# Six small reorderings in a diffusion-transformer layer: a load on another queue, three pieces of work on another engine or copied first, two steps turned later

## The chip, the core and the metric

The kernel runs on one core of a Trainium2 chip. The metric is the device time of one execution in microseconds (us), the median of repeated runs; lower is better. The engines are TensorE (PE in the profile, its weight loads PEld), VectorE (DVE), ScalarE (ACT), GpSimd (POOL) and SyncE (SP, which here only issues DMAs). L12 is line 12 of the kernel.

## What is computed

One layer for 1024 latent tokens and 256 context tokens of width 1024, in float32:

```python
h_lat = rms_norm(x, norm1_g) * (1.0 + sc1) + sh1        # sc1, sh1, ... = silu(c) @ w_mod + b_mod
h_ctx = rms_norm(ctx, norm1_g) * (1.0 + csc1) + csh1
p = h @ w_in                                            # 7 blocks of 512 columns
# retention: 4 heads of 128, both directions, chunks of 128, state carried from chunk to chunk
scores = (qc @ kc.T) * intra; o = scores @ vc + (qc * q_dec) @ S; S = S * c_dec + (kc * k_dec).T @ vc
# differential attention: 4 heads, two maps of 64; keys are the context and the latent tokens (1280)
a = softmax(q1 @ k1.T) - lam * softmax(q2 @ k2.T); y = subln(a @ v)
x = x + g1 * (concat(silu(rg) * ret, y) @ w_out)
u = conv3(h2 @ w_up); a, b = split(u); x = x + g2 * ((silu(a) * b) @ w_down)   # d_ff 2816, taps along the tokens
return rms_norm(x, final_g)
```

## The kernel before

Every matmul of a projection is done in three passes on values split into a high part (rounded to the faster format fp32r) and the remaining low part: high by high, high by low, low by high (`passes`, L131 to L133). The high part is cast by ScalarE, the low part is a subtraction, mostly on VectorE. In some stretches (the opening, the attention) the order of each engine's instructions is that of the code (`in_order`); elsewhere a scheduler orders them by readiness, and `order_only` adds a fixed precedence of one instruction to another of the same engine. In a queue a waiting instruction holds all behind it.

**Opening.** The rows of x come in on one DMA queue or another (`load_row`), the modulation weights in pieces (`mod_load`, tile wt), the projection's weights by blocks of two 128-row slices (`w_load`, tile raw, split by `w_split` into whi and wlo). A row is squared on ScalarE, its factor raised to −1/2 on GpSimd (`power`), scaled on VectorE (`scale`, L542), turned by TensorE into pt (L548), and `modulate(xs, d, ...)` writes the high part on ScalarE (L551), a temporary on VectorE (L553) and the low part (L555) for the 128-row slice d. `mod_part`, `mod_row` and `mod_sums` make the modulation itself: products into pr (L520), and small sums into pm and mcol. `part_products(ts, k)` multiplies slice k for the token tiles ts into pn. `turn_over(n)` issues n small products on ones (L606). Context tokens run through the same steps (cT).

**Retention.** `outputs()` is a generator that is run beside the q projection's products (pl, L131 to L133). A pair is two chunks of a head. In step n the pair n + 1 gets its scores, pair n its outputs (po) and the squares for its group norm (jk, ss on ScalarE, the power on GpSimd), pair n − 1 its gating (`gate`: four scalings o on VectorE, then y on GpSimd at L280 and L281), and pair n − 3 is turned by TensorE (`turn`: pyt, L286), split (yr) and stored (yrd, L291, on SP's queue). Behind the last y GpSimd issues the loads of the attention's operands (qhl, ks, va; L947 to L953).

**q items.** Each product block of q or k (bank pl) goes through `rotated`: ScalarE copies the two halves crosswise to xb (L423), VectorE multiplies pl by the cosine to xa (L425), then xb by the sine (L426, on GpSimd for the last items) and adds (L427). The attention is woven in before the last q items are done: scores pA (L868), row maxima on VectorE (L871), exponential on ScalarE (L875), transposes of p into pt (L888), which takes a bank of the same pool as pl, and copies aT (L894).

**Gated MLP.** Blocks j of 128 hidden columns are 2 by 2 products of Strassen's kind, accumulated in the bank `chain` in steps T2, T3, T4, with copies between them (ua at L1285, ub at L1293 and L1301, all on ScalarE); banks `second`, `third` and `fifth` hold further products. `combined(j)` makes the sums of weight tiles (cmb): s3 alone for the first blocks, on GpSimd (L1196). `conv` is the tap of width 3: the middle on ScalarE (L1238), the neighbours on VectorE (L1239, L1240), then SiLU (L1306). In blocks 1 to 3 (`late_gate`) the gating of the block before is issued after the middle of this one.

## Time and profile before

| | before |
|---|---|
| median of 3 runs | 1391.22 us (1389.7 to 1391.42) |
| profiled execution | 1391.29 us |
| its span, first to last instruction | 1389.5 us |
| mean granted TensorE clock | 0.998 |
| TensorE busy | 1363.6 us, 98% |
| VectorE, ScalarE, GpSimd busy | 996.3, 731.9, 306.2 us |

In rows of the timeline the first number is the start in us from the span's start, the second the length, then engine, line, operation and tiles; x6 after a row says that six such instructions run there one after the other; the bracket holds the idle time before the row and what ended it.

### The profile page before, as it was taken

The numbers are of one execution on the slowest core, as the hardware profiler recorded it, in microseconds if no ns is written. First come the engines' busy times: TensorE is split into PE (matmuls) and PEld (weight loads), VectorE is DVE, ScalarE is ACT, GpSimd is POOL, SyncE is SP. The second block draws the span as 40 slices with busy tenths as digits, with TensorE's granted clock in tenths as the row PEclk, the third lists the DMA queues.
The fourth block names the chain that finished last, engine by engine and source line by source line (L and its number), as shares of the span: only waits on it lengthen the run. The fifth ranks groups of instructions, "written<-read, shape, count | busy, mean of one in ns | idle before, by whom it ended". The sixth has DMA issues, their size and how long they took to land. (4 is left out here: it accounts for less than half of the span.)

```text
span 1389.5 us, 19442 instructions
## 1 busy us (share of the span) xinstructions
PE 1363.6 (98%) x7038; PEld 1145.9 (82%) x7038; DVE 996.3 (72%) x1464; ACT 731.9 (53%) x1395; POOL 306.2 (22%) x327
## 2 busy tenths in 40 slices
PE   8999999999999999999999999999999999999997
PEld 5788888888888899998887788888888888888886
DVE  4656773424776798895458998888778877798757
ACT  4652222424665789987136654555544555455542
POOL 1310000002655424411201643222332220000001
PEclk9999999999999999999999999999999999999999
DMA  9546885464454778622410232332322325963523
GB/s 367 207 167 214 286 280 180 142 178 141 152 187 149 205 178 184 139 51 99 171 64 23 99 113 100 114 114 93 112 104 109 114 75 177 371 220 104 175 91 129
DMA packets 94760, 214.61 MB, mean 154 GB/s; under 512 B 9221, under 2 KB 29189, under 8 KB 94153
## 3 DMA queue, kind: packets, MB, share of 16 engines
q1 hardware_dynamic: 85928, 186.64, 39.1%
q0 software_dynamic: 8160, 24.91, 7.9%
q10 hardware_dynamic: 576, 1.84, 0.4%
q8 instruction: 55, 0.90, 0.3%
q14 instruction: 41, 0.33, 0.1%
HBM read 158.03 MB, written 55.31 MB: 154 GB/s over the span
## 5 line engine op out<-in xcount | busy, mean ns | idle before, releaser
L131 PE MATMUL pl<-hT,whi 128*128 128x512 f32 x256 | 105.7, 413 | 0.0
L131 PE MATMUL chain<-T,whi 128*128 128x512 f32 x264 | 103.0, 391 | 1.2 <-ACT ub L1293 0.8
L132 PE MATMUL chain<-T,whi 128*128 128x512 f32 x264 | 102.7, 389 | 0.0
L133 PE MATMUL chain<-T,wlo 128*128 128x512 f32 x264 | 102.4, 389 | 0.0
L133 PE MATMUL pl<-hT,wlo 128*128 128x512 f32 x256 | 100.3, 392 | 0.3 <-DVE wlo L188 0.3
L132 PE MATMUL pl<-hT,whi 128*128 128x512 f32 x256 | 100.0, 391 | 0.0
L871 DVE TENSOR_REDUCE mt<-pA 128x1 f32<-128x1280 f32 x64 | 95.1, 1490 | 3.7 <-PE pA L868 2.3
L131 PE MATMUL c<-whi,ghl 128*128 128x512 f32 x232 | 90.2, 389 | 0.0
L132 PE MATMUL c<-wlo,ghl 128*128 128x512 f32 x232 | 90.2, 389 | 0.0
L133 PE MATMUL c<-whi,ghl 128*128 128x512 f32 x232 | 90.2, 389 | 0.0
L868 PE MATMUL pA<-ks,qhl 128*128 128x512 f32 (+1 forms) x384 | 89.5, 369 | 0.3 <-ACT p L875 0.3
L875 ACT ACTIVATE p<-pA,mt 128x1280 f32<-128x1280 f32 x64 | 85.5, 1336 | 6.2 <-DVE mt L871 6.1
L1039 ACT CAST whi<-cmb 128x512 fp32r<-128x512 f32 x62 | 38.5, 622 | 80.5 <-PE chain L132 63.0
L868 PEld LDWEIGHTS pA<-ks,qhl 128*128 128x128 f32 x384 | 67.7, 189 | 12.7 <-ACT p L875 1.0
L900 PE MATMUL pv<-va,aT 128*128 128x128 f32 x640 | 77.0, 275 | 0.1
L131 PE MATMUL pn<-whi,hT 128*128 128x512 f32 x188 | 76.8, 408 | 0.0
L1199 POOL TENSOR_TENSOR cmb<-wrb 128x512 f32<-128x512 f32 x19 | 27.6, 1452 | 221.9 <-DMA wrb<-w_up 132.0
L1042 DVE TENSOR_TENSOR wlo<-cmb,whi 128x512 fp32r<-128x512 f32 x62 | 61.0, 985 | 20.4 <-ACT whi L1039 20.4
L133 PE MATMUL pn<-whi,hT 128*128 128x512 f32 x188 | 73.7, 392 | 1.3 <-POOL hT L555 1.2
L900 PEld LDWEIGHTS pv<-va,aT 128*128 128x128 f32 x640 | 74.0, 192 | 0.7 <-DVE yT L929 0.3
L132 PE MATMUL pn<-wlo,hT 128*128 128x512 f32 x188 | 73.7, 392 | 0.8 <-DVE wlo L578 0.8
L1039 ACT CAST whi<-wra 128x512 fp32r<-128x512 f32 x55 | 33.8, 623 | 74.5 <-PE third L132 42.3
(326 smaller groups left out, 3824.3 us busy)
## 6 DMA issues: line engine op xcount, KB each, us to landing
wm<-w_mod SPq DMA_DIRECT2D x32, 512.0 KB, 5.3
raw<-w_in SPq DMA_DIRECT2D x27, 512.0 KB, 4.6
wra<-w_up SPq DMA_DIRECT2D x24, 512.0 KB, 3.3
wrb<-w_up SPq DMA_DIRECT2D x22, 512.0 KB, 3.5
W<-w_down SPq DMA_DIRECT2D x44, 256.0 KB, 6.0
ad<-s SPq DMA_DIRECT2D x20, 512.0 KB, 3.6
wra<-ad SPq DMA_DIRECT2D x20, 512.0 KB, 3.8
kvs<-kvg SPq DMA_DIRECT2D x36, 256.0 KB, 3.0
```

Source lines behind the costliest of these rows:

```text
L131: mm(ps, lh, rh, start=first, stop=False, skip_group_check=more)
L132: mm(ps, lh, rl, start=False, stop=False, skip_group_check=more)
L133: mm(ps, ll, rh, start=False, stop=last, skip_group_check=more)
L868: mm(self.pa[m][:, c0:c1], self.q[:, m, i, qs], self.k[:, m, c0:c1], start=(i == 0), stop=(i == 1))
L871: nc.vector.tensor_reduce(out=self.mt[:, m : m + 1], in_=self.pa[m][:, :LK], axis=AX.X, op=ALU.min)
L875: nc.scalar.activation(self.p[m], self.pa[m][:, :LK], AF.Exp, scale=-1.0, bias=self.mt[:, m : m + 1], accum_out=self.s[:, m : m + 1])
L900: mm(self.pv, self.aT[:, c, :], self.v[:, c, :], start=(c == 0), stop=(c == NKT - 1))
L1039: cast = nc.scalar.copy(hi, src)
L1042: nc.vector.tensor_tensor(out=lo, in0=src, in1=r32(hi), op=ALU.subtract)
L1199: nc.gpsimd.tensor_tensor(out=s1, in0=b1, in1=b2, op=ALU.add)
```

## The change

Six edits. (1) In the opening, row 1 of x goes to SP's queue and the first half of the projection's first weight block to ScalarE's; rows are scaled in two pieces of 3/4 and 1/4; the slices after the first are multiplied pass by pass over two token tiles, as the first was; the splits of weights stand ahead of the squares of the second group of rows; the count of small filler products changes. (2) The low part of slice 1 is made on VectorE, not GpSimd, for latents and context. (3) `turn` stands one step later in `outputs()`, behind the pair's outputs and squares, and the last one two steps later still. (4) The last q item's bank is copied whole by ScalarE into an SBUF tile before it is rotated. (5) s3 of block 1 is made on VectorE. (6) In blocks 1 to 3 the first tap of the gating is ordered behind the copy of the third chain step.

```diff
@@ outputs()
-                if 0 <= n - 3 < n_pairs:
-                    pairs[n - 3].turn()
                 if 0 <= n < n_pairs:
                     pairs[n].output(1)
                     pairs[n].squares()
                 yield
+                if n == n_pairs + 2:
+                    yield
+                    yield
+                if 0 <= n - 3 < n_pairs:
+                    pairs[n - 3].turn()
                 if 0 <= n - 1 < n_pairs:
                     pairs[n - 1].gate()
@@ rotated()
             xb = ev.tile([P, 512], F32, name="xb")
+            if eng is nc.gpsimd and (h, hf) == by_head[-1]:
+                held = ev.tile([P, 4, P], F32, name="st").rearrange("p h e -> p (h e)")
+                nc.scalar.copy(held, pt)
+                pt = held
@@ modulate()
-                eng = nc.gpsimd if d % 2 else nc.vector
+                eng = nc.gpsimd if d % 2 and d > 1 else nc.vector
@@ part_products()
-                if k > 0:
-                    for t in ts:
-                        passes(part[t], lat_lhs(t, k), wget(k, 0, 512), False, k == KD - 1)
-                    return
                 hi, lo = wget(k, 0, 512)
...
@@ opening
-            for t in range(2):
-                load_row(t, nc.scalar)
+            load_row(0, nc.scalar)
+            w_load(0, 0, 1, nc.scalar)
+            nc.sync.dma_start(out=ident, in_=consts[:, K_ID : K_ID + P])
+            load_row(1)
             mod_load(0, 1)
-            nc.sync.dma_start(out=ident, in_=consts[:, K_ID : K_ID + P])
-            w_load(0, 0, 1)
...
-            turn_over(2)
+            turn_over(9)
             mod_part(0, 1)
...
-            mod_row(0)
-            mod_sums(0)
-            scale(xs0[0], 2)
-            turn_over(6)
+            scale(xs0[0], 2, 0, 3 * P)
             square(xs0[1], 3)
             power(3)
+            mod_row(0)
             w_split(0, 1, nc.scalar)
-            scale(xs0[1], 3, 0, 2 * P)
+            scale(xs0[1], 3, 0, 3 * P)
+            mod_sums(0)
+            turn_over(1)
...
                 if k == 1:
                     mod_sums(2)
                     latents(0, 2)
+                    for t in (2, 3):
+                        scale(xs0[t], 2 + t, 3 * P, D)
...
+                if k in (0, 2, 4):
+                    w_split()
                 if k == 3:
                     square(xs1[0], 6)
                     square(xs1[1], 7)
...
-                if k in (0, 2, 4):
-                    w_split()
@@ combined()
-            nc.gpsimd.tensor_tensor(out=s3, in0=b2, in1=a1, op=ALU.subtract)
+            (nc.vector if j else nc.gpsimd).tensor_tensor(out=s3, in0=b2, in1=a1, op=ALU.subtract)
@@ conv() and gated()
-        def conv(u, idx):
+        def conv(u, idx, after=None):
...
-            nc.scalar.activation(t, u, AF.Identity, scale=w[1], bias=cl[:, COL_CB + idx : COL_CB + idx + 1])
+            mid = nc.scalar.activation(t, u, AF.Identity, scale=w[1], bias=cl[:, COL_CB + idx : COL_CB + idx + 1])
+            if after is not None:
+                order_only(mid.ins, after.ins)
...
-                ta = conv(self.ua, self.j)
+                ta = conv(self.ua, self.j, after and copied[-1])
```

The line numbers of the new kernel lie 3 to 7 higher than those above. On TensorE, at the last two outputs of retention (po the outputs of the last pair, pl products of the q projection, pyt a turn), the order before is this:

```order
L263 MATMUL po<-S_3513,qq 128x128
L131 MATMUL pl<-hT_167,whi 128x512
L132 MATMUL pl<-hT_169,whi 128x512
L133 MATMUL pl<-hT_167,wlo 128x512
L286 MATMUL pyt<-ident,y 128x128 x2
L262 MATMUL po<-kvo,sc 128x128
L263 MATMUL po<-S_3512,qq 128x128
```

and now:

```order
L131 MATMUL pl<-hT_167,whi 128x512
L132 MATMUL pl<-hT_169,whi 128x512
L133 MATMUL pl<-hT_167,wlo 128x512
L262 MATMUL po<-kvo,sc 128x128
L263 MATMUL po<-S_3515,qq 128x128
L262 MATMUL po<-kvo,sc 128x128
L263 MATMUL po<-S_3516,qq 128x128
L131 MATMUL pl<-hT_167,whi 128x512
L132 MATMUL pl<-hT_169,whi 128x512
L133 MATMUL pl<-hT_167,wlo 128x512
L286 MATMUL pyt<-ident,y 128x128 x2
```

The turn that stood ahead of the pair's second outputs stands three products behind them. Of the turns that follow, 15, 12 and 15 products stood before, between and ahead of the last one, 42 behind the last po in all; now it is 3, 15, 12 and 18, 48 in all: the last turn stands six products later.

On ScalarE, at the last q item (xb are the crossed halves, p the exponential of an attention unit, aT the copy of a transposed p), before:

```order
L875 ACTIVATE p_4291,sa<-pA,mt 128x1280
L410 CAST xhl<-xa 128x512
L423 ACTIVATE xb<-pl 64x512 x2
L875 ACTIVATE p_4293,sa<-pA,mt 128x1280
L894 COPY aT<-pt 128x512
```

and now:

```order
L880 ACTIVATE p_4294,sa<-pA,mt 128x1280
L413 CAST xhl<-xa 128x512
L427 COPY st<-pl 128x512
L430 ACTIVATE xb<-st 64x512
L880 ACTIVATE p_4296,sa<-pA,mt 128x1280
L430 ACTIVATE xb<-st 64x512
L899 COPY aT<-pt 128x512
L880 ACTIVATE p_4460,sa<-pA,mt 128x1280
```

The copy st reads the bank pl whole; one half of xb moves behind the exponential.

On ScalarE, in blocks 0 and 1 of the MLP (chain 7398 is block 0's, 7458 block 1's, 7526 block 2's; in the new order 7403, 7463 and 7531), before:

```order
L1301 COPY ub_7675<-chain_7398 128x512
L1039 CAST whi_7896<-wra_7780 128x512
L1285 COPY ua_7523<-chain_7458 128x512
L1238 ACTIVATE tconv_7771<-ub_7675,cl_63 128x1024
L1306 ACTIVATE tconv_7767<-tconv_7767 128x1024
L1238 ACTIVATE tconv_7865<-ua_7523,cl_63 128x1024
L1293 COPY ub_7712<-chain_7458 128x512
```

and now:

```order
L1308 COPY ub_7680<-chain_7403 128x512
L1044 CAST whi_7901<-wra_7785 128x512
L1292 COPY ua_7528<-chain_7463 128x512
L1044 CAST whi_7917<-wra_7785 128x512
L1300 COPY ub_7717<-chain_7463 128x512
L1243 ACTIVATE tconv_7772<-ua_7460,cl_63 128x1024
L1243 ACTIVATE tconv_7776<-ub_7680,cl_63 128x1024
L1044 CAST whi_7937<-x1_7_6694 128x512
L1308 COPY ub_7717<-chain_7463 128x512
L1044 CAST whi_7953<-x1_7_6694 128x512
L1313 ACTIVATE tconv_7772<-tconv_7772 128x1024
L1190 COPY ua_7796<-chain_7531 128x512
```

Block 0's taps and its SiLU now stand behind block 1's copies, and block 2's first copy behind the SiLU. On TensorE five products of block 2's chain stood between the second and the third step of block 1's chain (T20, T21 and T30 are factors of the second and third step):

```order
L133 MATMUL chain_7458<-T20_7385,wlo_7732 128x512
L131 MATMUL chain_7526<-T20_7385,whi_7813 128x512
L132 MATMUL chain_7526<-T21_7386,whi_7813 128x512
L133 MATMUL chain_7526<-T20_7385,wlo_7814 128x512
L131 MATMUL chain_7526<-T20_7385,whi_7813 128x512
L132 MATMUL chain_7526<-T21_7386,whi_7813 128x512
L131 MATMUL chain_7458<-T30_7387,whi_7749 128x512
```

and now there is none:

```order
L132 MATMUL chain_7463<-T21_7391,whi_7736 128x512
L133 MATMUL chain_7463<-T20_7390,wlo_7737 128x512
L131 MATMUL chain_7463<-T30_7392,whi_7754 128x512
L132 MATMUL chain_7463<-T31_7393,whi_7754 128x512
L133 MATMUL chain_7463<-T30_7392,wlo_7755 128x512
```

Block 2's five products moved behind the whole of block 1's third and fourth step.

More of the change, by code (lines that the diff above doesn't have):

```diff
@@ L563, in wget, with w_load @@
                 return tuple(t[:, k % 2, c0:c1] for t in sl[k // 2])
-            def w_load(kk, i0=0, i1=2):
+            def w_load(kk, i0=0, i1=2, eng=nc.sync):
                 if i0 == 0:
                     raws.append(wr.tile([P, 2, 512], F32, name="raw"))
-                nc.sync.dma_start(out=raws[-1][:, i0:i1], in_=w_in[6][:, 2 * kk + i0 : 2 * kk + i1, :])
+                eng.dma_start(out=raws[-1][:, i0:i1], in_=w_in[6][:, 2 * kk + i0 : 2 * kk + i1, :])
             def w_split(i0=0, i1=2, only=None):
@@ L589, in part_products @@
             def part_products(ts, k):
-                if k > 0:
-                    for t in ts:
-                        passes(part[t], lat_lhs(t, k), wget(k, 0, 512), False, k == KD - 1)
-                    return
                 hi, lo = wget(k, 0, 512)
                 for t in ts:
-                    mm(part[t], lat_lhs(t, k)[0], hi, start=True, stop=False)
+                    mm(part[t], lat_lhs(t, k)[0], hi, start=(k == 0), stop=False)
                 for t in ts:
                     mm(part[t], lat_lhs(t, k)[0], lo, start=False, stop=False)
-                if 3 in ts:
+                if k == 0 and 3 in ts:
                     latents(0, 1)
                 for t in ts:
-                    mm(part[t], lat_lhs(t, k)[1], hi, start=False, stop=False)
+                    mm(part[t], lat_lhs(t, k)[1], hi, start=False, stop=(k == KD - 1))
             def turn_over(n):
@@ L636 @@
             power(2)
-            mod_row(0)
-            mod_sums(0)
-            scale(xs0[0], 2)
-            turn_over(6)
+            scale(xs0[0], 2, 0, 3 * P)
             square(xs0[1], 3)
             power(3)
+            mod_row(0)
             w_split(0, 1, nc.scalar)
-            scale(xs0[1], 3, 0, 2 * P)
+            scale(xs0[1], 3, 0, 3 * P)
+            mod_sums(0)
+            turn_over(1)
             w_split(0, 1, nc.vector)
             square(xs0[2], 4)
-            power(4)
             latents(0, 0, 0, 2)
             square(xs0[3], 5)
+            power(4)
+            scale(xs0[0], 2, 3 * P, D)
             power(5)
+            scale(xs0[1], 3, 3 * P, D)
+            scale(xs0[2], 4, 0, 3 * P)
+            scale(xs0[3], 5, 0, 3 * P)
             for q in range(2):
@@ L658 @@
                     mod_row(1)
-                    scale(xs0[2], 4, 0, 2 * P)
-                    scale(xs0[3], 5, 0, 2 * P)
                     latents(0, 0, 2, 4)
@@ L685 @@
                 if k == 0:
-                    for t in range(1, 4):
-                        scale(xs0[t], 2 + t, 2 * P, D)
                     for q in range(2):
```

## The prediction

> **What bounds the kernel now.** I read the page first, its busy shares and the chain that ended last:

> ```profile
> PE 1363.6 (98%) x7038; PEld 1145.9 (82%) x7038; DVE 996.3 (72%) x1464; ACT 731.9 (53%) x1395; POOL 306.2 (22%) x327
> PE 40%; DVE 2%; ACT 0%; issue 0%; DMA 0%; POOL 0%; POOLq 0%; ACTq 0%
> ```

> TensorE is busy in 1363.6 of 1389.5 us, so 25.9 us is all that any change of order could remove, and no edit here takes a matmul away. What can move is TensorE's idle time. The second view is therefore the waits of PE by releaser (columns: who waited for whom, total us, times, longest):

> ```profile
> PE pyt L286 <- POOL y L281: 1.6, 1, 1.6
> ...
> PE pt L1086 <- DVE x L1081: 1.3, 1, 1.3
> PE pn L133 <- POOL hT L555: 1.2, 1, 1.2
> ...
> PE pu L328 <- ACT jk L271: 1.1, 1, 1.1
> PE pt L888 <- DVE xa L425: 0.9, 1, 0.9
> PE chain L131 <- ACT ub L1293: 0.8, 1, 0.8
> ...
> PE pn L132 <- DVE wlo L578: 0.8, 1, 0.8
> ```

> Each edit sits at one of these lines. Their sum, with 0.3 of a second chain wait below, is 8.0 us: the ceiling of the change. Whether a wait goes or only changes its name is the whole question, so the third view is the timeline around each. All sums are made against the profiled execution's own 1391.29 us, which lies 0.07 above the median of 1391.22. A difference of 0.2%, 2.8 us, is about what a measurement of this kernel can tell from none.

> **Opening (edits 1 and 2).** The DMA share is the last but one column here (16 engines, 1.00 is all of them busy), and the timeline rows are start, length, engine, operation, then the idle time before it:

> ```profile
> 12.00:24.00 12.00, 9.29 (x67) 5.50 (x66) 8.44 (x18) 6.15 (x11) 3.29 (x4) 1.00 1.02 411
> 24.00:36.00 12.00, 12.00 (x98) 8.65 (x99) 6.27 (x13) 4.34 (x7) 1.29 (x1) 1.00 1.00 387
> ```

> ```profile
> 21.17 1.57 POOL L555 TENSOR_TENSOR hT<-tmp,hT 128x512 fp32r<-128x512 f32 x1 [5.33 <-DVE tmp L553]
> 22.80 0.50 PE L133 MATMUL pn<-whi,hT 128*128 128x512 f32 x1 [1.24 <-POOL hT L555]
> 26.90 0.69 DVE L555 TENSOR_TENSOR hT<-tmp,hT 128x512 fp32r<-128x512 f32 x1
> 42.52 1.07 PE L520 MATMUL pr<-wt,cz 128*32 128x256 f32 x16
> 49.79 1.04 PE L548 MATMUL pt<-ident,xs 128*128 128x128 f32 x8
> ```

> The low part of column block 1 takes 1.57 on POOL and 0.69 on DVE: the wait of 1.24 goes. Against it, DVE now does that subtraction in the stretch where it also scales rows, and part of the scaling stands ahead of row 2's and 3's first transposes; I put 0.5 on the path, so 0.7 is won by 23 us. Swapping queues for row 1 and the first weight block moves no byte away: DMA is full from 12 to 36, so the modulation weights that TensorE multiplies at 42.52 cannot come sooner by what the matmuls save. Later the split of weights moves ahead of the squares; the 0.76 wait for wlo then goes, but the transposes at 49.79 still need row sums, power and scaling, which are now later by the length of that split. I count nothing there. With two context subtractions put on DVE the sum is 0.2 lower still. **−0.5; ends −1.4 (both waits go, less half of the 1.24 as new scaling) and +0.5 (only the added DVE work counts).**

> **Last turn of retention (edit 3).** Rows around it, and the loads of the attention that POOL issues right behind the last y (from the DMA view of 440 to 456: count, KB each, median us from issue to landing):

> ```profile
> 441.05 0.73 POOL L281 TENSOR_TENSOR y<-y,kvo 128x256 f32<-128x256 f32 x1
> 441.71 2.58 POOL L947 DMA_DIRECT2D qhl<-dq  x4
> 441.83 0.44 PE L286 MATMUL pyt<-ident,y 128*128 128x128 f32 x2 [1.63 <-POOL y L281]
> 444.26 2.11 POOL L950 DMA_DIRECT2D ks<-dk  x4
> 454.36 1.40 PE L868 MATMUL pA<-ks,qhl 128*128 128x512 f32 x6
> ks<-dk POOLq DMA_DIRECT2D x4, 320.0 KB, 10.2
> ```

> In the new order six more products stand ahead of the last transpose. From the chain rows further down, 17 products and a wait of 0.85 fill 788.62 to 793.63, so one is 0.24 and six are 1.4: nearly all of 1.63 would be covered. But y itself ends at 441.78 as before, since its chain of copy, squares, power and gate is not shortened, and the loads are issued behind it. Issued at 444.26 to 446.37 with 10.2 to land, the first keys land at about 454.4, and TensorE starts on them at 454.36 without a wait. TensorE would come to that place 1.4 sooner and wait there for the keys. Only what y gains by having one DVE add of the earlier turn behind the gates, and the spread of the landings, is left. **−0.4; ends −1.6 and 0.** The other turns move as well. Of SP's queue the stores of a turned pair (yrd) stand later, one of them now ahead of the weight load whose lateness gives the 1.1 of pu; either could shift it. **0; ends −1.1 (that wait goes) and +0.8 (a store that waits holds the load).**

> **Last q item (edit 4).**

> ```profile
> 466.76 1.20 ACT L423 ACTIVATE xb<-pl 64x512 f32<-64x512 f32 x2 [1.26 <-PE pl L133]
> 467.98 1.33 ACT L875 ACTIVATE p<-pA,mt 128x1280 f32<-128x1280 f32 x1
> 467.99 0.69 DVE L425 SCALAR_TENSOR_TENSOR xa<-pl,rtab 128x512 f32<-128x512 f32 x1 [0.73 <-ACT xb L423]
> 468.74 0.88 PE L888 MATMUL pt<-ident,p 128*128 128x128 f32 x6 [0.93 <-DVE xa L425]
> 469.45 1.43 PE L868 MATMUL pA<-ks,qhl 128*128 128x512 f32 x6
> 471.58 1.43 PE L868 MATMUL pA<-ks,qhl 128*128 128x512 f32 x6 [0.26 <-ACT p L875]
> ```

> The bank that pt needs is freed by xa at 468.68. A copy of the whole bank first (the same shape as the chain copies below, 0.59) frees it at 467.35, so 0.93 goes. But the scores at 469.45 need the banks that the exponential of 467.98 empties, at 469.31; the copy takes the place of half of xb ahead of it, so that exponential is no sooner, and TensorE stands there instead. The other half of xb, 0.60, now stands behind it and ahead of the next exponential, whose end the scores at 471.58 already wait for (0.26). ACT, not the bank, paces this place. **+0.5; ends −0.9 (the wait goes and no scores are held) and +0.9 (0.60 and 0.26 both count).**

> **s3 of block 1 (edit 5).**

> ```profile
> 747.08 1.27 POOL L1196 TENSOR_TENSOR cmb<-wrb,wra 128x512 f32<-128x512 f32 x1
> 747.15 1.48 DVE L1081 TENSOR_SCALAR x<-x,sm 128x512 f32<-128x512 f32 x1 [0.67 <-POOL sm L114]
> 748.69 0.33 PE L1086 MATMUL pt<-ident,x 128*128 128x128 f32 x1 [1.32 <-DVE x L1081]
> 749.15 0.48 DVE L1081 TENSOR_SCALAR x<-x,sm 128x512 f32<-128x512 f32 x1
> ```

> The scaling takes 1.48 beside POOL's subtraction and 0.48 without it. On DVE the subtraction (0.69, as the other of its kind above) fits into the 0.67 in which DVE waited for the power anyway, and the scaling ends 1.0 earlier; 0.3 of the wait stays. [...] **−1.0; ends −1.3 (the whole wait) and −0.5 (half, if DVE's split behind it becomes late).**

> **Taps (edit 6).**

> ```profile
> 787.45 0.63 ACT L1039 CAST whi<-wra 128x512 fp32r<-128x512 f32 x1
> 787.98 0.59 ACT L1285 COPY ua<-chain 128x512 f32<-128x512 f32 x1
> 788.62 0.50 PE L131 MATMUL chain<-T,whi 128*128 128x512 f32 x1 [0.31 <-ACT ua L1285]
> 791.73 1.29 POOL L1202 TENSOR_TENSOR wrb<-wra,cmb 128x512 f32<-128x512 f32 x1
> 791.74 2.35 DVE L1239 SCALAR_TENSOR_TENSOR tconv<-ub,cl,tconv 128x1023 f32<-128x1023 f32 x1
> 793.01 0.56 ACT L1293 COPY ub<-chain 128x512 f32<-128x512 f32 x1
> 793.63 0.50 PE L131 MATMUL chain<-T,whi 128*128 128x512 f32 x1 [0.85 <-ACT ub L1293]
> 797.07 1.28 DVE L1239 SCALAR_TENSOR_TENSOR tconv<-ua,cl,tconv 128x1023 f32<-128x1023 f32 x1
> ```

> Before, the copy at 793.01 stood behind ACT's tap; ordered first, and with five products of another bank between, it is hidden and 0.85 goes. But five products of another bank also stood ahead of T3 at 788.62, and these are moved away: T3 now follows T2 of the same bank directly. Behind the end of block 0's T4 ACT has a copy, a cast and a copy (0.59 + 0.63 + 0.59 = 1.8), TensorE only four products, 0.9: a wait of 0.9 in place of 0.31. Block 2's first sum now stands behind SiLU, which waits for DVE's taps: I put 0.2 there, near nothing, because sixteen products of other banks stand ahead of the place. The sum is 0.9 + 0.2 − 0.31 − 0.85 = **−0.1; ends −1.0 (both copies hidden) and +0.8 (SiLU 0.9 later than I have it).**

> **Sum:** −0.5 − 0.4 + 0 + 0.5 − 1.0 − 0.1 = −1.5, 1391.29 − 1.5 = **1389.8**. If every part came at its upper end the sum would be +2.5, at its lower −7.3; with independent errors most of it lies within 2 of the middle.

> **Rivals.** *Every wait simply goes*: POOL's y 1.6, s3 1.3, the exponential that costs nothing 0.9, both chain copies 1.0, the opening 0.8: −5.6, **1385.7**. For it: TensorE's queue does have other work at each place in the new order, and the key loads may land sooner than their median says. Against it: 454.36 follows the loads too closely, and ACT is the later of two at 468. *All are replaced*: opening 0, turn 0, q item +0.9, s3 −0.5, taps +0.8: +1.2, **1392.5**; the change then does not do what its orders say. For it: three of the new waits have a row above. *Slower*: VectorE's taps of block 0 fall beside POOL's sums. A tap takes 2.35 beside POOL at 791.74 and 1.28 alone at 797.07, so four of them cost 4 × 1.07 = 4.3 ahead of SiLU, of block 2's first sum and of TensorE: 1389.8 + 4.3 = **1394.1**. It decides if POOL's four sums are still running when the taps start; against it, the taps move later and the last sum starts at 791.73, before them. [...]

> **How the numbers follow.** Forecast 0.45, every wait goes 0.28, all replaced 0.17, slower 0.10. Faster by over 0.2% is below 1388.4: the second case and a seventh of the first, 0.34. Slower is above 1394.0: the last case and 0.01 of the third, 0.11. The rest, 0.55, is within 0.2%. For 8 in 10 the range takes in 1385.7 with a little below, the forecast and 1392.5: 1385.5 to 1392.8. It leaves out the last case and tails.

> **What would show it.** Right: in the waits of PE, y L281, x L1081 and hT L555 are gone or under 0.4, and pA L868 waits about 1.2 for the DMA of ks; the scores after the last q item start 0.5 later against their exponential; chain waits some 0.9 for ua. Wrong: pA starts 1.4 earlier without a wait (then the turn is won whole), or L1246 and L1247, the taps, show over 2 us each beside POOL, and a wait of chain for ua of several us. If the first 60 us end over 1.4 earlier, the bytes were not what held them.

## The result and the profile after

The changed kernel takes 1399.26 us (median of 4 runs, 1398.63 to 1401.61), the kernel before 1390.58 in its 4 runs (1389.7 to 1391.42): 1.0066 times as long, 95% interval 1.0048 to 1.0083. Forecast were 1389.8 and a range up to 1392.8. The profiled execution took 1398.63 us with a span of 1396.9, at a mean granted clock of 0.996 where before had 0.998.

First the busy shares, from the page of the changed kernel:

```profile
PE 1367.9 (98%) x7042; PEld 1148.3 (82%) x7042; DVE 998.2 (71%) x1469; ACT 730.6 (52%) x1396; POOL 303.2 (22%) x323
```

TensorE has the same matmuls (4 instructions more of 7042) and yet is busy 4.3 us longer: part of the loss is no wait at all, but matmuls that ran slower. The rest is in the waits of PE by releaser:

```profile
PE pt L893 <- ACT aT L899: 2.7, 2, 2.1
PE pyt L286 <- DVE yr L289: 2.1, 1, 2.1
PE chain L131 <- ACT ua L1292: 1.8, 2, 1.1
PE pyt L286 <- POOL y L281: 1.8, 1, 1.8
PE pA L873 <- ACT p L880: 1.7, 2, 1.0
PE pA L873 <- DMA ks<-dk: 1.4, 1, 1.4
...
PE chain L131 <- ACT ua L1190: 1.1, 1, 1.1
...
PE pt L1091 <- DVE x L1086: 0.5, 1, 0.5
```

Gone are the waits for GpSimd's hT, for wlo, jk, xa L425 and ub; y is still there with 1.8, where it was to go; six waits are new or longer. Where they cost time is seen by setting the start of each matmul against the start of the same matmul before. The difference of the starts, and by how much it steps at each place:

| place (us of before) | lag behind before, after the place | step | predicted |
|---|---|---|---|
| opening, to 60 | −0.5 (−0.6 at 395) | −0.5 | −0.5 |
| 406, a turn in the middle of retention | +1.6 | +2.2 | 0 |
| 441, the last turns | +1.8 | +0.2 | −1.6 |
| 454, first scores of the attention | +3.2 | +1.4 | +1.2 |
| 466 to 485, last q item | +6.7 | +3.5 | +0.5 |
| 748, s3 of block 1 | +5.9 | −0.75 | −1.0 |
| 786 to 860, taps | +8.7 | +2.75 | −0.1 |

(1.6 sooner to the keys and 1.2 of wait for them were together the −0.4 of the last turn.) From there the lag stays at 8.67 to the last matmul; the span grows by 7.4, since the stretch behind the last matmul is 1.3 shorter.

**406.** The timeline (start, length, engine, line, operation, idle time before and its releaser):

```profile
405.58 1.04 ACT L187 CAST whi<-raw 128x1024 fp32r<-128x1024 f32 x1 [4.98 <-DMA raw<-w_in]
406.66 1.23 DVE L188 TENSOR_TENSOR wlo<-raw,whi 128x1024 fp32r<-128x1024 f32 x1 [2.13 <-ACT whi L187]
406.84 0.35 ACT L288 CAST yr<-pyt 128x256 fp32r<-128x256 f32 x1
407.80 0.42 DVE L289 TENSOR_TENSOR yr<-pyt,yr 128x256 fp32r<-128x256 f32 x1
408.37 0.41 PE L286 MATMUL pyt<-ident,y 128*128 128x128 f32 x2 [2.12 <-DVE yr L289]
```

ScalarE stands 4.98 at the cast of a weight slice whose load has not landed. Behind it on ScalarE stands the cast that reads the last turn's bank, and behind the slice's split on VectorE the subtraction that frees it. The next turn needs that bank and waits 2.12. The load is hardly later (the slice's cast starts at 405.58, and at 405.52 before); it is the turn's cast that now stands behind it. Before, the turn of this place ran at 405.80 without a wait and TensorE lost 1.11 to jk a little later. Then something new shows in the windows (start:end, length, busy time of PE, PEld, DVE, ACT, POOL, the granted clock, the DMA share, GB/s):

```profile
409.00:410.00 1.00, 1.00 (x5) 0.75 (x4) 0.07 (x1) 0.42 (x1) 0.98 (x1) 0.62 0.59 210
411.00:412.00 1.00, 1.00 (x6) 0.90 (x6) 1.00 (x4) 0.94 (x6) 0.29 (x1) 0.50 0.00 0
413.00:414.00 1.00, 1.00 (x10) 1.00 (x9) 0.68 (x2) 0.95 (x3) 0.92 (x2) 1.00 0.00 0
```

From 409.2 on TensorE's clock is granted at half for 3.4 us; 6 matmuls run in the microsecond from 411, 10 in that from 413 at full clock, and one of 512 columns follows another by 0.42 or 0.43 (409.42 to 410.69), where it is 0.23 at full clock (415.70 to 415.93). That is the other part of the +2.2.

**441.** The last pair's y, on ScalarE and GpSimd:

```profile
434.36 0.57 ACT L267 COPY o<-po 128x512 f32<-128x512 f32 x1
435.72 0.38 PE L286 MATMUL pyt<-ident,y 128*128 128x128 f32 x2
436.49 0.37 ACT L288 CAST yr<-pyt 128x256 fp32r<-128x256 f32 x1 [1.12 <-DVE o L278]
439.15 0.30 ACT L272 ACTIVATE ss<-ss,geps 128x4 f32<-128x4 f32 x1
444.20 0.72 POOL L281 TENSOR_TENSOR y<-y,kvo 128x256 f32<-128x256 f32 x1
447.41 2.11 POOL L955 DMA_DIRECT2D ks<-dk  x4
457.32 1.40 PE L873 MATMUL pA<-ks,qhl 128*128 128x512 f32 x6 [1.44 <-DMA ks<-dk]
```

The cast yr of the moved turn now stands among the pair's squares; it waits 1.12, and the squares behind it wait with it. The row names VectorE's o. But the transposes that the cast reads had ended at 436.10, and yr is a tile with one buffer (`bufs=1`), which is free only when the store of the turn before has landed. That store was issued at 433.13, and the DMA view has 3.3 from issue to landing for it, so it landed at 436.4, just ahead of the cast:

```profile
yrd<-yr SPq DMA_DIRECT2D x1, 256.0 KB, 3.3
```

From the copy o to the sum ss that was, in the trace of before,

```profile
432.07 0.59 ACT L267 COPY o<-po 128x512 f32<-128x512 f32 x1
435.51 0.30 ACT L272 ACTIVATE ss<-ss,geps 128x4 f32<-128x4 f32 x1
```

3.44 us, and is now 439.15 − 434.36 = 4.79. The last y ends at 444.92, where it ended at 441.78 before. Of these 3.14, 1.6 is the lag from 406; the copy o starts 0.69 later beyond that lag, the squares take 1.35 more, and the steps behind ss 0.50 less. With y the loads of the attention leave later, and the first scores wait 1.44 for their keys.

**Last q item.**

```profile
472.71 0.63 ACT L430 ACTIVATE xb<-st 64x512 f32<-64x512 f32 x1
472.98 1.55 DVE L888 SCALAR_TENSOR_TENSOR p<-p,r,p 128x1280 f32<-128x1280 f32 x1
473.48 2.16 POOL L433 TENSOR_TENSOR xb<-xb,rtab 128x512 f32<-128x512 f32 x1 [3.55 <-ACT xb L430]
475.68 0.59 ACT L899 COPY aT<-pt 128x512 f32<-128x512 f32 x1 [2.34 <-POOL xb L433]
476.32 0.66 PE L893 MATMUL pt<-ident,p 128*128 128x128 f32 x4 [2.13 <-ACT aT L899]
```

The second half of xb stands behind the exponential, so GpSimd's sine product cannot start before 473.4; the copy aT, which reads only pt, waits 2.34 for that product, and TensorE 2.13 for aT. Together with 1.04 and 0.66 for the exponential and another stretch at half clock (478.00 to 481.00 was granted 0.51; worth about 1.2, an estimate, since six products pA take 2.50 in it where they take 1.45 at 472.74, and four transposes 1.06 where they take 0.66 at 476.32), and less the 0.93 and 0.26 that stood here before, this is 3.8, near the +3.5.

**Taps.** The first sums of a chain step on TensorE, and ScalarE at the second of them:

```profile
794.23 0.50 PE L131 MATMUL chain<-T,whi 128*128 128x512 f32 x1 [1.12 <-ACT ua L1292]
820.62 0.50 PE L131 MATMUL chain<-T,whi 128*128 128x512 f32 x1 [1.07 <-ACT ua L1190]
846.09 0.50 PE L131 MATMUL chain<-T,whi 128*128 128x512 f32 x1 [0.68 <-ACT ua L1292]
```

```profile
819.04 1.06 ACT L1313 ACTIVATE tconv<-tconv 128x1024 f32<-128x1024 f32 x1 [1.77 <-DVE tconv L1247]
820.00 0.57 ACT L1190 COPY ua<-chain 128x512 f32<-128x512 f32 x1
```

Block 3's first copy stands behind the SiLU, and the SiLU waits 1.77 for VectorE's taps. A wait costs more than its listed length, which begins at the modelled end of the last matmul: the 1.07 moves the lag by 1.4, the 0.68 by 1.0.

### The profile page after: what moved, and what is told of

Same layout as the page of the kernel before. It is cut to its first block, busy times and chain, and to the rows that moved or that the text cites. A ratio compares the mean times of both kernels' runs of the same rounds, so it can differ in the third digit from the quotient of the medians.

```text
span 1396.9 us, 19458 instructions
## 1 busy us (share of the span) xinstructions
PE 1367.9 (98%) x7042; PEld 1148.3 (82%) x7042; DVE 998.2 (71%) x1469; ACT 730.6 (52%) x1396; POOL 303.2 (22%) x323
## 3 DMA queue, kind: packets, MB, share of 16 engines
q10 hardware_dynamic: 576, 1.57, 0.3%
## 4 chain that ended last, share of the span: by engine, by line
PE 88%; DVE 4%; ACT 3%; DMA 2%; issue 2%; POOL 1%; SPq 0%; POOLq 0%; ACTq 0%; DVEq 0%
PE chain L131 6%; PE chain L132 5%; PE chain L133 5%; PE pv L905 5%; PE pA L873 5%; PE c L132 5%; PE c L133 5%; PE c L131 5%; PE pn L133 3%; PE pn L131 3%; PE pn L132 3%; PE pl L133 3%; PE pl L132 3%; PE pl L131 3%; PE third L133 3%; PE third L131 3%
## 5 line engine op out<-in xcount | busy, mean ns | idle before, releaser
L131 PE MATMUL pl<-hT,whi 128*128 128x512 f32 x256 | 106.7, 417 | 0.0
L131 PE MATMUL chain<-T,whi 128*128 128x512 f32 x264 | 103.6, 393 | 2.9 <-ACT ua L1292 1.8
L132 PE MATMUL chain<-T,whi 128*128 128x512 f32 x264 | 102.8, 389 | 0.0
L133 PE MATMUL chain<-T,wlo 128*128 128x512 f32 x264 | 102.6, 389 | 0.0
L133 PE MATMUL pl<-hT,wlo 128*128 128x512 f32 x256 | 100.7, 394 | 0.2 <-DVE wlo L188 0.2
L132 PE MATMUL pl<-hT,whi 128*128 128x512 f32 x256 | 100.4, 392 | 0.0
L131 PE MATMUL c<-whi,ghl 128*128 128x512 f32 x232 | 90.2, 389 | 0.0
L132 PE MATMUL c<-wlo,ghl 128*128 128x512 f32 x232 | 90.2, 389 | 0.0
L133 PE MATMUL c<-whi,ghl 128*128 128x512 f32 x232 | 90.2, 389 | 0.0
L1047 DVE TENSOR_TENSOR wlo<-cmb,whi 128x512 fp32r<-128x512 f32 x62 | 55.4, 896 | 25.3 <-ACT whi L1044 25.1
L131 PE MATMUL third<-yT,whi 128*128 128x512 f32 x168 | 65.4, 389 | 0.0
L132 PE MATMUL third<-yT,whi 128*128 128x512 f32 x168 | 65.4, 389 | 0.0
L133 PE MATMUL third<-yT,wlo 128*128 128x512 f32 x168 | 65.3, 389 | 0.0
```

The costliest lines, as they stand in the source:

```text
L131: mm(ps, lh, rh, start=first, stop=False, skip_group_check=more)
L132: mm(ps, lh, rl, start=False, stop=False, skip_group_check=more)
L133: mm(ps, ll, rh, start=False, stop=last, skip_group_check=more)
L1047: nc.vector.tensor_tensor(out=lo, in0=src, in1=r32(hi), op=ALU.subtract)
```

## The experiments

All kernels but one were timed in 5 rounds against the kernel before, whose medians in these four groups were 1390.3 to 1390.9. Each ratio is to that. The theory was that three of the edits cost time apart from each other, each by an instruction on ScalarE or GpSimd that a moved step put ahead of another; the rivals were that the losses share a cause, so that undoing one brings back less or more than its step of the table, or that each place waits for something else as soon as its wait is gone.

**One edit undone.** Three kernels are the changed one without edit 3, 4 or 6; a fourth, called rest, has edits 1, 2 and 5 alone.

no_turn:

```diff
+                if 0 <= n - 3 < n_pairs:
+                    pairs[n - 3].turn()
                 if 0 <= n < n_pairs:
...
-                if n == n_pairs + 2:
-                    yield
-                    yield
-                if 0 <= n - 3 < n_pairs:
-                    pairs[n - 3].turn()
```

> The new kernel with the turn of a pair put back to its old place (edit 3 undone). Theory, from the two traces: the turn cost 2.2 us at 406 (a wait of 2.1 for yr where 1.1 stood for pu, and half the TensorE clock for 3 us after it), 0.2 at 443 and 1.4 at the key loads, 3.8 in all; then this kernel takes about 1399.3 - 3.8 = 1395.5 and shows no halved clock near 410. Rival: the turn's lag only moved the phase of the loads, and the weight load that comes late at 405 gives the same long wait without it; then 1398 or more and the halved clock stays.

1395.79, ratio 1.0034 (1.0022 to 1.0045). The wait for yr is gone, and one of 0.6 for jk is in its place; the wait for aT is still there with 2.2. The mean granted clock of the profile is 0.996, as with the whole change.

no_held:

```diff
-            if eng is nc.gpsimd and (h, hf) == by_head[-1]:
-                held = ev.tile([P, 4, P], F32, name="st").rearrange("p h e -> p (h e)")
-                nc.scalar.copy(held, pt)
-                pt = held
```

> The new kernel without the copy of the last q item's bank (edit 4 undone). Theory: the copy cost 3.5 us (waits of 1.0, 2.1 and 0.7 around 472 to 477 and half the clock from 477.6 to 481); then about 1395.8, with one wait of about 0.9 for xa in its place. Rival: the lag of the key loads from edit 3 is what pulls these waits apart; then 1398 or more, with waits over 2 us near 475 still there.

1396.55, ratio 1.0038 (1.0025 to 1.0051). The waits of aT shrink to 0.6 and the old one is back:

```profile
PE pt L889 <- DVE xa L428: 0.9, 1, 0.9
PE pt L889 <- ACT aT L895: 0.6, 1, 0.6
```

The wait for yr at 406 is 1.8 here. The mean granted clock of the profile is 0.999, where before has 0.998, so no half clock shows behind that wait.

no_taps:

```diff
-                ta = conv(self.ua, self.j, after and copied[-1])
+                ta = conv(self.ua, self.j)
```

> The new kernel with the taps not ordered behind the chain's copies (edit 6 undone). Theory: the order cost 2.75 us from 786 to 866 (waits of chain for ua of 1.1, 1.1 and 0.7 against 0.3 and 0.85 before); then about 1396.5, with the old two waits. Rival: s3 on VectorE, not the order, delays VectorE's taps and so SiLU; then 1398.5 or more and a wait for the copy at L1190 stays.

1397.16, ratio 1.0048 (1.0035 to 1.0061). The wait for the copy at L1190 is gone, and the old ones of 0.3 and 0.8 are back.

rest: the three of them together.

> Only the opening, the low part of slice 1 on VectorE and s3 of block 1 on VectorE (edits 1, 2 and 5; edits 3, 4 and 6 undone). Theory: the parts add up, -0.5 by 60 us and -0.75 at 750, so about 1389.3 against 1390.6, faster by 0.1%. Rival: the opening's gain is given back at 406, where the weight load comes late anyway; then 1390.0 or more.

1388.83, ratio 0.9989 (0.9980 to 0.9997): faster. Its long waits stand where before had them, without GpSimd's hT:

```profile
PE pyt L286 <- POOL y L281: 1.7, 1, 1.7
PE pu L328 <- ACT jk L271: 1.1, 1, 1.1
```

From the ratio 1.0066 of the whole change, undoing the turn wins 0.0032, the copy 0.0028 and the order of the taps 0.0018, in us of before 4.4, 3.9 and 2.5; together 10.8. The whole change and rest lie 0.0077 or 10.7 apart. Each ratio is known to about 0.001, so this sum could be off by some 6 us, and an agreement within 0.1 is luck. The profiles say the same, though: against the changed kernel the last matmul comes 3.8, 4.3 and 2.2 sooner without the turn, the copy and the order, 10.3 together, and 9.6 sooner in rest. So the three losses add, as far as this can tell, and edits 1, 2 and 5 are a gain of some 1.5.

**The q item: which wait is it?** On rest, with edit 4 put back. In h_tile the copies aT come from a pool whose tiles wait only for the readers of what they overwrite, not for all readers of the pools whose memory it takes over:

```diff
+            if eng is nc.gpsimd and (h, hf) == by_head[-1]:
...
-        at = p2.enter_context(tc.tile_pool(name="at", bufs=2))
+        at = p2.enter_context(tc.tile_pool(name="at", bufs=2, reuse_waits="tile"))
```

> Edits 1, 2, 5 and the copy of the last q item (edit 4), and the pool that holds aT waits for its own memory only, so that the first aT no longer waits for GpSimd's sine product of the last q item. Theory: that wait, 2.1 us on TensorE, and the halved clock behind it were what the copy cost; without it only ACT's pacing is left, some 0.5, so about 1388.8 + 0.5 = 1389.3, no wait over 1.1 near 470 and no slow steps after it. Rival: the copy and the exponential's new place cost by themselves; then 1391.5 or more.

1389.69, ratio 1.0000 (0.9991 to 1.0009), 0.9 above rest (1.2 by the lag of the matmuls in the profiles). GpSimd's product is as late and long as in the changed kernel, but aT no longer waits for it, and no half clock follows (six products pA take 1.41 at 476.31, as at full clock):

```profile
469.36 0.59 ACT L896 COPY aT<-pt 128x512 f32<-128x512 f32 x1
469.48 2.16 POOL L430 TENSOR_TENSOR xb<-xb,rtab 128x512 f32<-128x512 f32 x1 [3.34 <-ACT xb L427]
473.35 0.66 PE L890 MATMUL pt<-ident,p 128*128 128x128 f32 x4 [0.60 <-ACT aT L896]
```

The wait was therefore not for the data of aT, but for the place in memory. What is left is the exponential that stands behind the copy, for which the prediction had +0.5 and at most +0.9.

In h_first both halves of xb stand ahead of the exponential:

```diff
+            if eng is nc.gpsimd and (h, hf) == by_head[-1]:
...
+        order_only(units[1].ex.ins, last_xb[0].ins)
```

> Edits 1, 2, 5 and the copy of the last q item (edit 4), with both crossed halves ordered ahead of the next exponential; aT still waits for GpSimd's sine product. Theory: the sine product then starts some 2.1 us earlier than with the copy alone, before VectorE's combine, so aT waits little: about 1389.5 to 1390.0. Rival: the sine product stays slow beside VectorE, or the later exponential costs as much; then 1391.5 or more.

1388.43, ratio 0.9989 (0.9980 to 0.9998), no worse than rest. There is one wait now, for the later exponential, and GpSimd's product runs beside no combination of VectorE:

```profile
PE pA L872 <- ACT p L879: 1.7, 1, 1.7
```

```profile
469.76 1.26 POOL L432 TENSOR_TENSOR xb<-xb,rtab 128x512 f32<-128x512 f32 x1 [1.88 <-ACT xb L429]
```

So 1.26 is the product without a combination beside it, and 2.16 the product beside VectorE's 1.55.

**The turn: the step or the delay of the last?** On rest, t_step turns a step later without the two extra yields, t_last delays only the last turn.

```diff
-                if n == n_pairs + 2:
-                    yield
-                    yield
```

> Edits 1, 2, 5 and the turn one step later, without the two last steps of delay for the last turn. Theory: the loss at 406 belongs to the step (the next turn needs the bank that yr empties, and yr stands behind the cast that waits for the late weight load): a wait of 1.8 to 2.1 there with the halved clock behind it, and 1 to 2 us at the end of the retention; about 1388.8 + 3.5 = 1392.3. Rival: the delayed last turn is what costs, through the key loads; then under 1390.

1393.59, ratio 1.0021 (1.0013 to 1.0030).

```profile
PE pyt L286 <- POOL y L281: 3.1, 1, 3.1
PE pyt L286 <- DVE yr L289: 2.2, 1, 2.2
...
PE pA L866 <- DMA ks<-dk: 0.8, 1, 0.8
```

Against rest its matmuls fall back by 2.4 at 406 (wait and half clock, less the 1.1 of jk), 1.5 at 441 and 1.0 at the first scores: 4.9.

```diff
+                if n == n_pairs + 2:
+                    yield
+                    yield
                 if 0 <= n - 3 < n_pairs:
                     pairs[n - 3].turn()
```

> Edits 1, 2, 5 and only the delay of the last turn by two steps; all other turns in their old place. Theory: y is no earlier, so most of the wait for y, 1.6, becomes a wait for the key loads: 0.7 less for y (three products more ahead of it), 0.5 more for ks, about 1388.6 (-0.2). Rival: the key loads were no limit; then 1388.1 or less and no wait for ks.

1388.95, ratio 0.9992 (0.9983 to 1.0001).

```profile
PE pyt L286 <- POOL y L281: 0.9, 1, 0.9
```

The wait falls from 1.7 to 0.9, but the lag against rest goes from −0.3 behind it to +0.1 at the first scores, which start at 453.35, as in rest at 453.34. No wait for the keys is listed there (the gap is 0.14), so that the keys hold them is argued from the equal starts. The delay costs nothing and wins nothing; the step is what costs.

**406: the order on ScalarE.** t_yr is t_step with the last slice's cast and split ordered behind the eighth turn's yr:

```diff
+        for half, turn in zip(halves[-1], turns[7]):
+            order_only(half.ins, turn.ins)
```

> The turn one step later (edits 1, 2, 5 and the step of edit 3), with the cast and the split of the last weight slice of the block ordered behind the cast and the subtraction of the eighth turn. Theory: TensorE waited 2.2 us at 406 because yr stood behind the cast of a weight slice that landed late; with yr ahead of it the bank is free, the long wait and the halved clock go, and 1.3 to 2.4 us of the 4.8 that the step cost come back: 1391.2 to 1392.3. Rival: the late weights hold the products or the keys' state updates there as well; then 1393 or more, with another wait of 2 us at 406.

1393.3, ratio 1.0021 (1.0013 to 1.0030): no better in sum. At 406 the loss is gone (its lag against rest moves by 0.06 there), so the place behaves as said. But at 441 TensorE waits longer for y and now half clock follows (445.00 to 449.00 was granted 0.57):

```profile
PE pyt L287 <- POOL y L282: 3.6, 2, 3.3
```

That eats most of the gain: apart from its opening, which was slower (the mean granted clock of the profile is 0.995, t_step's 0.997), the profile is 1.2 ahead of t_step's, and the medians are 0.3 apart.

t_sq also orders the thirteenth turn's cast yr behind the last squares:

```diff
+        order_only(turns[12][0].ins, squared[0].ins)
```

> The turn one step later as in the kernel with yr ahead of the late weight slice, and the thirteenth turn's yr ordered behind the last pair's squares. Theory: the 2.7 us lost at 441 came from ScalarE waiting at that yr in the middle of the squares, 1.1 of idle and 0.4 of work, which sets the last y and with it the key loads; about 1.5 come back: 1391.8. Rival: the last y is late because its outputs are; then 1393 or more.

1401.08, ratio 1.0069 (1.0056 to 1.0083): a miss. At its own place it does what was expected: from o (435.63) to ss (439.05) 3.42 pass, as before the change, and y's wait falls from 3.3 to 1.5. But a q product's bank now comes free late, and TensorE stands there longer than anywhere else:

```profile
PE pl L131 <- DVE xa L425: 5.9, 1, 5.9
```

The trace shows what holds that rotation. ScalarE stands 9.90 at the cast of the last turn, for the store of the turn before, which was issued at 450.91; the crossed halves xb are queued behind that cast:

```profile
461.55 0.37 ACT L289 CAST yr<-pyt 128x256 fp32r<-128x256 f32 x1 [9.90 <-DMA yrd<-yr]
```

So here too the one buffer of yr is what a moved turn runs into. No run gave yr a second one. That yr among the squares lengthens y's chain is shown by the 3.42; that this is the whole loss at 441 stays open.

**406: the load.** The slice that ScalarE waits for can also come sooner. after_raw is the whole change with that load issued on SP's queue ahead of one of the loads of kvo; raw_early is the same on h_first.

```diff
+        order_only(kvo_dma[12].ins, raw_dma[0].ins)
```

> The whole new kernel, with the load of the block's last weight slice issued ahead of the kvo load that waits for GpSimd's y. Theory: the slice lands some 2 to 4 us earlier, ScalarE does not stand at its cast, yr empties the bank in time, and the wait of 2.1 at 406 with the halved clock behind it goes: 2.3 less by 430; of that, what the last y does not give back: 1396.5 to 1398. Rival: the bank is late for another reason; then 1399 and the wait stays.

1399.86, ratio 1.0063 (1.0050 to 1.0076): no gain, against what was expected. The 2.12 is gone from the trace, as the theory has it, and the lag against the changed kernel falls by 2.6 there, more than that wait. But y (1.9), aT (2.1) and the taps are as they were, the keys wait 0.9, the mean granted clock is 0.994 where the changed kernel has 0.996, and the profiled execution lost 2.5 in the opening. The cause holds at its place; that its removal shortens the whole is not shown with the other losses present.

> Edits 1, 2 and 5, the copy with both crossed halves ahead of the exponential, and the last weight slice's load issued ahead of the kvo load. Theory: the wait of 1.1 for pu at 406 goes without moving any cast: 1387.4. Rival: the loads behind it come later by as much, or the last y, whose chain does not move, takes it back; then 1388.4.

1387.0 (1386.51 to 1390.05), ratio 0.9975 (0.9963 to 0.9986): the fastest of all, faster than before and after, and 1.4 below h_first. The two intervals overlap; but the executions with a mean clock of 0.998 or more took 1386.51 to 1387.03 here (five) and 1387.28 to 1388.43 in h_first (six). The wait for jk at 406 is gone, its lag against rest falls there by 1.5, and 1.0 is lost again at the first scores, 0.8 of it as a wait for the keys.

combo tries the same place on h_first by order, the slice's cast behind the ninth turn's yr:

```diff
+        for half, turn in zip(halves[-1], turns[8]):
+            order_only(half.ins, turn.ins)
```

> Edits 1, 2 and 5, the last q item's copy with both crossed halves ahead of the exponential, and the last weight slice's cast and split ordered behind the ninth turn. Theory: the wait of 1.1 at 406, which comes from ScalarE standing at that cast, goes, and the weights are still in time: about 1388.4 - 1.0 = 1387.4, the fastest so far. Rival: TensorE then waits for the weights, or the turns get later; then 1388.4 or more.

1388.54, ratio 0.9985 (0.9976 to 0.9994), as h_first; 1387.4 was expected. The wait has moved to the products that need the slice:

```profile
PE pl L131 <- ACT whi L189: 1.5, 1, 1.5
```

**The taps.** taps_first is rest with edit 6, and with the SiLU of blocks 0 to 2 ordered behind the first copy of two blocks on:

```diff
+        for i in range(3):
+            order_only(silus[i].ins, firsts[i + 2].ins)
```

> Edits 1, 2, 5 and the order of the taps (edit 6), with SiLU of blocks 0 to 2 ordered behind the first copy of the block two further on. Theory: of the 2.75 us that the order cost, the 1.1 at 819 and most of the 0.7 at 845 came from that copy standing behind SiLU, which waits for VectorE's taps; they go and the 1.1 at 793 stays: about 1388.8 + 1.0 = 1389.8. Rival: the waits belong to VectorE's taps themselves; then 1391 or more.

1391.49, ratio 1.0004 (0.9995 to 1.0013); 1389.8 was expected. The wait at 819 is gone, so the SiLU ahead of the copy was its cause. The other stays, and a new one of 1.3 comes at 856, again for a copy behind a SiLU:

```profile
PE chain L131 <- ACT ua L1287: 2.4, 2, 1.3
```

In the profiles the taps cost 1.7 where they cost 2.75. The medians do not show this: taps_first lies 0.0015 or 2.1 us above rest, where the order cost 2.5. The 1.12 is, as the prediction argued, the price of having T3 directly behind T2; no run took that away.

**The clock.** clock repeats a chain copy in the MLP of the kernel before, 5 to 10 times in blocks 5 to 20, to make waits of graded length:

```diff
+                for _ in range(1 + {5: 5, 6: 6, 7: 7, 8: 8, 9: 5, 10: 6, 11: 7, 12: 8, 13: 9, 14: 6, 15: 7, 16: 8, 17: 9, 18: 9, 19: 10, 20: 10}.get(j, 0)):
+                    self.copied = nc.scalar.copy(self.ua[:, 512:], self.chain)
```

> The kernel before, with the copy of the chain bank after its second step repeated 6 to 11 times in blocks 5 to 20 of the MLP; the repeats write the same values again, and TensorE has to wait for them. One look at the length of a wait and the clock behind it, 16 waits of 0.5 to 4 us in otherwise full stretches. Theory, from the runs so far: a wait of 2.1 us or more is followed within some 3 us by a stretch of about 3.4 us at half the clock, one under 1.8 never is, and in between it depends on where the wait falls. Rival: only the long idle share of the attention's stretch around it does it; then no halved clock here at any length.

Executed once: 1403.23, at a mean granted clock of 0.996. Only one long wait for the copy arose, of 2.0 (three come to 2.8). This doesn't show what length of a wait is followed by half clock.

## Why the prediction was wrong

**Right: the opening (1, 2) and s3 (5).** The opening is −0.5, as forecast, but in part by luck. It was ahead by 1.0 at 38, where 0.7 was forecast for 23, and gave half of that back by 60, where about nothing was counted: wlo's 0.76 went, but transposes waited for VectorE, 0.49 for the scaling at 48.92 and 0.79 for a temporary at 55.34. That the full DMA held it is not shown, and no run took edits 1 and 2 apart. s3: the scaling now takes 0.44 (two in 0.88, at 748.79), the wait falls from 1.32 to 0.5, and −0.75 is won where −1.0 was forecast.

**Right by luck: the keys.** The first scores wait 1.44 where about 1.2 was forecast, and the loads are issued behind y, as said. But in the forecast TensorE came 1.4 sooner to keys that land as before; in the run TensorE came 1.8 later, and the keys later still, since y was 3.14 later (the landing takes 9.7 where it took 10.2).

**Wrong: y "ends at 441.78 as before, since its chain of copy, squares, power and gate is not shortened".** It was not shortened, but lengthened: the part from the copy to ss by 1.35 (4.79 against 3.44), and with it y ends 1.54 later than the lag of 1.6 explains. Step 3 counted the turn's transposes and its store's place in SP's queue, but not its cast, which is queued on ScalarE among the squares of the last pair, the very chain on which y hangs, and which needs the buffer that the store before it empties. So the 1.6 that six products were to hide was lost again.

**Wrong: the other turns, 0 with the ends −1.1 and +0.8.** The step looked at SP's queue, and put +0.8 to a store that holds the load; the load was not held. The price is on ScalarE and VectorE: the reader of the turned bank fell behind a weight cast that waits 4.98 for its load, and the 1.1 of jk became 2.1 of yr, and the rest of the 2.2, some 1.2, is the clock's. That wait of ScalarE for raw was in the trace of before too, with 3.48 and the yr behind it at 408.67; there, a turn that needed the bank was not due so soon.

**Wrong: the q item, +0.5.** The mechanism named (the exponential later by the copy) is there, 1.04 and 0.66, and h_tile prices it at 0.9 in the medians, the upper end. What was not seen is a dependence that is no data: the first tiles of a pool laid over released memory wait for the last readers of what lay there. xb was one, and the change made it late. Before, GpSimd's product ended ahead of the first aT and this wait had no length.

**Wrong: the taps, −0.1.** The 0.9 for T3 came as 1.12, and ub's 0.85 went, as written. The "0.2, near nothing" for SiLU was the term that was mis-sized: not at block 2, where it was put, but at block 3 with 1.07, and 0.68 at the third step of a later block. The order was repeated in three blocks, and only the first was gone through.

**The rivals.** The slower case came in its sign, but not by its mechanism. It needed taps beside GpSimd's sums; block 0's taps took 1.28 each:

```profile
799.34 1.28 DVE L1246 SCALAR_TENSOR_TENSOR tconv<-ua,cl,tconv 128x1023 f32<-128x1023 f32 x1 [0.33 <-ACT tconv L1243]
```

*All are replaced* named the right kind of outcome for the turn and the q item, and gave +1.2 in sum for +8.7. The range was too narrow since each term was bounded by the wait that was visible, and no term by the engine queue into which a moved instruction falls.

## What to carry to other kernels

Follow every instruction of a moved step on every engine, not only the matmuls that it frees: ask what stands ahead of its cast on ScalarE, what chain now has to pass it, and what must land before its one buffer is free. A wait that is replaced by a longer one can cost twice on TensorE, once as idle time and once in clock (at 406, 2.1 for 1.1 and some 1.2 more at half clock). And where a pool is laid over released memory, the last reader of that memory is a dependence of the first tile, however unrelated its data (here 2.34 us for aT).

## What the hardware showed

```profile
446.00:447.00 1.00, 1.00 (x5) 0.81 (x4) 0.96 (x2) 0.00 (x0) 1.00 (x3) 0.50 0.13 39
```

```profile
446.00:447.00 1.00, 1.00 (x6) 0.78 (x6) 0.70 (x2) 0.23 (x1) 1.00 (x3) 1.00 0.57 76
```

**The same in the opening.** In h_first's profile a stretch at half clock of 6.8 us begins at 11.7 us (0.84 granted from 11 to 12, 0.50 from 12 to 18, 0.74 from 18 to 19), in rest's none. In h_first and in rest, in this order:

```profile
12.00:15.00 3.00, 2.35 (x9) 1.75 (x9) 2.03 (x7) 2.54 (x5) 0.00 (x0) 0.50 1.02 413
```

```profile
12.00:15.00 3.00, 2.13 (x11) 1.38 (x11) 2.47 (x8) 2.50 (x5) 0.35 (x1) 1.00 1.02 414
```

A good part of the spread of the times of one kernel can come from this: of rest's 11 timed executions, the eight with a mean clock of 0.998 or 0.999 took 1387.38 to 1389.06, the three with 0.995 or 0.996 took 1390.55 to 1391.54; of h_first's 11, the six with 0.998 or 0.999 took 1387.28 to 1388.43, the five with 0.996, the profiled one among them, 1389.77 to 1390.94. Medians of many runs are needed to see a change of 1 us. Why one execution has such a stretch and another has not was not shown.
